# A four-layer fp32 step on one core: the last block's second half of columns gated during the first product, scaling by ScalarE, modulation in smaller turns

## The chip, the core and the metric

The kernel runs on one core of one Trainium2 chip. The metric is device time in microseconds. TensorE (PE in the profile) multiplies matrices out of SBUF into PSUM; VectorE (DVE) and ScalarE (ACT) read and write SBUF and PSUM; GpSimd (POOL) does small things and issues some DMAs; SyncE (SP) issues most DMAs from one queue, in order.

## The reference

One inference step of a backbone of four layers on 128 context tokens and 512 latent tokens, width 1024, in float32. Layer l uses a mixer of kind l mod 3: gated linear attention (GLA, layers 0 and 3), a Conformer convolution (layer 1), a short gated convolution (layer 2). Every layer ends with an MLP.

```
for l in range(4):
    mp, ms = adaln(c_ctx, mod_w[l], mod_b[l]), adaln(c, mod_w[l], mod_b[l])   # 6 vectors of 1024 each: silu(c) @ w + b
    hp, hs = xp * (1 + mp[1]) + mp[0], xs * (1 + ms[1]) + ms[0]
    op, os = mixer_l(hp), mixer_l(hs)
    xp = layer_norm(ALPHA * xp + mp[2] * op);  xs = layer_norm(ALPHA * xs + ms[2] * os)
    fp = square(relu(modulate(xp, mp[3], mp[4]) @ w1[l])) @ w2[l]             # width 4096; the same for xs
    xp = layer_norm(ALPHA * xp + mp[5] * fp);  xs = layer_norm(ALPHA * xs + ms[5] * fs)
```

The outputs are both streams after the last layer and the final states of the GLA scan for the context.

## The kernel before

**Tokens and tiles.** The 640 tokens are five row tiles of 128 (`TT = 5`; tile 0 is the context), which stay in SBUF as `x[t]`. The input of a product stands transposed in `hT`, as two float32r parts, high and low; each weight is split the same way (`split`: a cast on ScalarE, L118, a subtraction on VectorE, L119), and a product is three matmuls, high by high, high by low, low by high. Weights come from HBM through `staged`: five staging buffers of 512 KB (pool `stage`), then the split into weight buffers (pool `wp`, and in a mixer also `wq`, three buffers of each part).

**Order.** PE's instructions run in the order in which the program issues them. The other engines' instructions, the DMA issues on SP among them, are put into a list by a scheduler that goes by the order of the program, readiness in a simulated time, and free buffers; on the chip each engine then runs its list in order. Waits are inserted where data or buffers ask for them.

**MLP.** The 4096 middle columns are done in four blocks `b` of 1024. For each, the first product makes `acts` (in blocks 1 to 3 by a scheme of seven products on half-size forms, `sevens`, L1315, whose forms are built by L118, L119 and L1287), and the second product multiplies them by a block of `w2`, in two halves of 512 columns, `n = 0, 1`. `mm2_wide` goes over a half with five PSUM banks at once, four weights by five row tiles: 20 slots of six matmuls, L208. The results are collected in `x[t]`, whose old value is saved in DRAM after the first block (`saved`). In the last block the epilogue `gathered` adds the collected sum (L264), multiplies by the gate (L265) and adds the saved x (L266), which a DMA on SP brings into one half of the tile `acc` (`room`, L263); the half is `t % 2`, so load t + 2 waits for the addition of tile t. In the last block `n = 0` runs in `mm2_wide`, `n = 1` in `mm2_part`, row tile by row tile (24 matmuls each, L231). The last layer has a plain epilogue, `residual` (L246, L247: multiply by the gate, add), and no saved x; so have the ends of the mixers.

**The norm and the next input.** Behind the epilogue of `n = 1`, `ln` takes the statistics of a row tile (L463, L464, L472, then POOL's L473, L474, L466), normalises the first half of the columns on VectorE (L510) and the second on ScalarE (L512), and registers the rest for 6.2 us of matmul time later (`LN_GAP`): `modulated` transposes the tile on PE (L494, two halves of four), scales it to the next layer's input, the first half on ScalarE (L501), the second on VectorE (L503), and splits it into `hT` (L483, L484).

**Modulation.** The vectors of the next layers are made beside the products. Some groups by PE (`mod_step`), the groups in `MOD_DVE` by VectorE (`mod_dve`): for one vector and one half of its columns, four steps `p`, each with one staged load that holds two k tiles, and per k tile two multiply-adds into `acc` (L400, or ScalarE's L398 at the first). After the last step PE sums over the partitions (L419) and turns the row (L371). Steps are taken by `tick`: some number of times in each `mm2_wide`, and after each group of `sevens`, by `STEPS[l]`; `drain` and `pause` take what is left ahead of a layer's end.

**Opening.** In layer 0 the first modulation comes in eight units (`unit`, two staged loads of 512 KB each); `part_sums` multiplies one (L574), its sums are copied out (L580) and turned (L602), and `products` does the k tile's part of the first GLA products (L679). Unit u + 2 is asked for when unit u has been read. Then come the weights `gvr` of the next products.

## Time and profile before

| | us |
|---|---|
| median of 3 runs | 3017.94 |
| lowest and highest | 3017.71, 3019.01 |
| profiled execution | 3019.96 |
| its span, first to last instruction | 3018.2 |
| mean granted clock of PE in it | 0.988 |

The busy times are shares of the span. The granted clock is a share of 2.4 GHz; PE runs at 1.2 or at 2.4 GHz, and a value between is a mean over a stretch. An idle time of PE with a name behind it is a wait; the name is that of the instruction that ended it. The profiled execution is 1.76 us longer than its span and 2.02 us longer than the median.

### The profile page before, as it was taken

How to read it: one execution, taken by the hardware profiler on the slowest of the kernel's cores; microseconds unless marked ns; L12 is line 12 of the kernel's file. 1: busy time of each engine (PE TensorE's matmuls, PEld its weight loads, DVE VectorE, ACT ScalarE, POOL GpSimd, SP SyncE). 2: the span in 40 equal slices, each digit the busy share in tenths (PEclk: the TensorE clock that was granted, in tenths of full speed). 3: DMA queues.
4: the chain of work that ended last, by engine and by line, in shares of the span. 5: the costliest groups of instructions: out<-in, count | busy, mean ns of one | idle time of the engine just before them, and what ended most of it. 6: DMA issues, size and time to landing. Idle time of an engine off the chain costs nothing.

```text
span 3018.2 us, 42986 instructions
## 1 busy us (share of the span) xinstructions
PE 2913.3 (97%) x16988; PEld 2551.2 (85%) x16988; DVE 2114.7 (70%) x3399; ACT 1212.6 (40%) x1974; POOL 204.3 (7%) x379
## 2 busy tenths in 40 slices
PE   7999999999999999999999999999999999999998
PEld 6788798888788698998889989888988887988996
DVE  4444779798787775776788578877775447685676
ACT  4333354352442353533533234534533443533442
POOL 0001100100110010000010010010010000000000
PEclk9999999999999999999999999999999999999999
DMA  6334244444455334323435324444333312212222
GB/s 248 122 123 157 74 161 136 156 136 162 161 161 148 110 112 139 110 90 124 149 115 170 101 70 142 135 140 133 115 117 128 105 57 74 87 67 84 91 70 77
DMA packets 110809, 366.46 MB, mean 121 GB/s; under 512 B 14996, under 2 KB 20796, under 8 KB 110608
## 3 DMA queue, kind: packets, MB, share of 16 engines
q1 hardware_dynamic: 98656, 333.92, 33.7%
q0 software_dynamic: 11952, 29.80, 3.1%
q8 instruction: 134, 2.20, 0.3%
q14 instruction: 67, 0.55, 0.1%
HBM read 348.55 MB, written 15.11 MB: 120 GB/s over the span
## 4 chain that ended last, share of the span: by engine, by line
PE 81%; DVE 11%; DMA 3%; ACT 2%; issue 2%; POOL 0%; SPq 0%; DVEq 0%; ACTq 0%; POOLq 0%
PE mx L208 14%; PE mm L231 11%; PE mm L208 9%; PE mx L165 9%; PE mx L1315 9%; PE mm L165 9%; PE mm L1315 6%; PE mx L231 5%; DVE acc L400 2%; DVE form L119 1%; DVE wlo L119 1%; PE mx L1090 1%; PE md L346 1%; DMA st<-in_w 1%; PE o L885 1%
## 5 line engine op out<-in xcount | busy, mean ns | idle before, releaser
L118 ACT CAST whi<-st 128x1024 fp32r<-128x1024 f32 (+1 forms) x262 | 273.9, 1050 | 654.8 <-PE mx L208 115.6
L119 DVE TENSOR_TENSOR wlo<-st,whi 128x1024 fp32r<-128x1024 f32 (+1 forms) x262 | 318.8, 1220 | 267.4 <-ACT whi L118 266.4
L208 PE MATMUL mx<-whi,act 128*128 128x512 f32 x1344 | 453.2, 391 | 0.0
L118 ACT CAST form<-st 128x512 fp32r<-128x512 f32 x336 | 201.1, 619 | 371.9 <-DVE st L1287 167.1
L208 PE MATMUL mm<-whi,act 128*128 128x512 f32 x896 | 313.6, 391 | 0.5 <-DVE x L247 0.5
L208 PEld LDWEIGHTS mx<-whi,act 128*128 128x128 f32 x1344 | 252.6, 188 | 57.6 <-issue 4.2
L231 PE MATMUL mm<-whi,hT 128*128 128x512 f32 x920 | 296.9, 395 | 0.0
L119 DVE TENSOR_TENSOR form<-st,form 128x512 fp32r<-128x512 f32 x336 | 224.9, 686 | 93.8 <-ACT form L118 93.4
L400 DVE SCALAR_TENSOR_TENSOR acc<-st,cm,acc 128x512 f32<-128x512 f32 x392 | 276.0, 746 | 19.3 <-ACT acc L398 13.6
L165 PE MATMUL mm<-hT,whi 128*128 128x256 f32 (+1 forms) x1264 | 277.7, 310 | 0.0
L165 PE MATMUL mx<-hT,whi 128*128 128x384 f32 (+1 forms) x1216 | 270.1, 311 | 4.2 <-ACT hT L483 2.4
L208 PE MATMUL mx<-wlo,act 128*128 128x512 f32 x672 | 262.1, 390 | 0.0
L1315 PE MATMUL mx<-hT,form 128*128 128x320 f32 x1428 | 232.3, 311 | 12.9 <-DVE form L119 6.1
L1315 PEld LDWEIGHTS mx<-hT,form 128*128 128x128 f32 x1428 | 215.0, 189 | 18.7 <-DVE form L119 8.8
L165 PEld LDWEIGHTS mm<-hT,whi 128*128 128x128 f32 x1264 | 211.7, 190 | 2.1 <-issue 1.0
L165 PEld LDWEIGHTS mx<-hT,whi 128*128 128x128 f32 x1216 | 205.2, 189 | 6.7 <-ACT hT L483 3.2
L208 PEld LDWEIGHTS mm<-whi,act 128*128 128x128 f32 x896 | 168.2, 188 | 37.5 <-issue 2.1
L231 PEld LDWEIGHTS mm<-whi,hT 128*128 128x128 f32 x920 | 171.5, 188 | 33.4
L165 PE MATMUL mm<-hT,wlo 128*128 128x256 f32 (+1 forms) x632 | 195.2, 309 | 0.5 <-DVE wlo L119 0.5
L165 PE MATMUL mx<-hT,wlo 128*128 128x384 f32 (+1 forms) x608 | 188.6, 310 | 0.0
L231 PE MATMUL mm<-wlo,hT 128*128 128x512 f32 x460 | 183.9, 400 | 0.0
L208 PE MATMUL mm<-wlo,act 128*128 128x512 f32 x448 | 174.8, 390 | 0.0
(313 smaller groups left out, 5183.8 us busy)
## 6 DMA issues: line engine op xcount, KB each, us to landing
st<-in_w SPq DMA_DIRECT2D x256, 512.0 KB, 3.4
st<-in_modv SPq DMA_DIRECT2D x112, 512.0 KB, 3.4
st<-in_modw SPq DMA_DIRECT2D x80, 512.0 KB, 4.5
st<-in_gvr SPq DMA_DIRECT2D x32, 512.0 KB, 5.1
st<-in_cpw SPq DMA_DIRECT2D x24, 512.0 KB, 5.7
st<-in_scin SPq DMA_DIRECT2D x24, 512.0 KB, 4.1
ur<-uscr SPq DMA_DIRECT2D x40, 238.0 KB, 5.4
st<-in_gqk SPq DMA_DIRECT2D x16, 512.0 KB, 5.3
```

Of the source, the lines that this page charges most:

```text
L118: self.nc.scalar.copy(hi, src)
L119: self.nc.vector.tensor_tensor(out=lo, in0=src, in1=hi.bitcast(F32), op=AL.subtract)
L165: self.nc.tensor.matmul(ps[:m, :n], w[a][:, kt * m:(kt + 1) * m], self.hT[:, h, kt, c0:c0 + n], start=(i == 0), stop=(i == 3 * KT - 1),)
L208: self.nc.tensor.matmul(ps[t], lhs(2 * i + k, h, t), s[a][:, k * 512:k * 512 + 512], start=(i == 0 and k == 0 and a == 0 and h == 0), stop ...
L231: self.nc.tensor.matmul(ps, lhs(kt, h, t), s[a][:, c + cols.start:c + cols.stop], start=(i == 0), stop=(i == 3 * nk - 1))
L346: nc.tensor.matmul(ps[32 * t:32 * t + 32, :], self.cm[:, kt, :], st[t // 2][:, c:c + 512], start=(kt == 0), stop=(kt == KT - 1),)
L400: nc.vector.scalar_tensor_tensor(out=acc[:, s], in0=w, scalar=c, in1=acc[:, s], op0=AL.mult, op1=AL.add)
L885: nc.tensor.matmul(o[t], Ep[i][:, t * 128:(t + 1) * 128], ss[i], start=False, stop=((m, i) in ((2, 1), (3, 0), (3, 1))))
L1090: nc.tensor.matmul(ps[32 * g:32 * g + 32, :5 * GRID], w[:, g, q], ur[i][:, g, :, 4 * q:4 * q + GRID], start=(q == 0), stop=(q == 7))
L1315: nc.tensor.matmul(ps, w[c][:, k * 128:(k + 1) * 128], x[:, h, k], start=(i == 0), stop=(i == 11))
```

## The change

1. In the last block of the MLPs of layers 0 to 2, the second half of the columns is gated early: `gather`, a generator stepped between the slots of the first half's `mm2_wide`, multiplies the collected sum of each row tile by the gate and adds the saved x. Behind the second half's product stands the plain epilogue. The first half keeps `gathered`.
2. In those MLPs ScalarE scales both halves of a row tile to the next layer's input (`by_act`).
3. A step of `mod_dve` takes one k tile (two multiply-adds) instead of two; there are eight to a half vector, every second one with a load. `STEPS` doubles, and the short convolution's `mm1` ticks twice for each tick before.
4. Units 1 to 7 of the opening are loaded into the weight buffers of `wq`, not into staging, and unit u + 3 is asked for when unit u has been read.

```diff
-STEPS = {0: (6, 1), 1: (3, 0), 2: (6, 0), 3: (0, 0)}
+STEPS = {0: (12, 2), 1: (6, 0), 2: (12, 0), 3: (0, 0)}
...
-                self.tick()
+                for _ in range(turns):
+                    self.tick()
...
+    def gather(self, saved, room):
+        nc = self.nc
+        c = slice(512, 1024)
+        for _ in range(7):
+            yield
+        for t in range(TT):
+            was, xs = room[:, t % 2], self.x[t][:, c]
+            nc.sync.dma_start(was, saved[t][:, c])
+            nc.vector.tensor_tensor(out=xs, in0=xs, in1=self.gate[:, 0 if t == 0 else 1, c], op=AL.mult)
+            nc.vector.tensor_tensor(out=xs, in0=xs, in1=was, op=AL.add)
+            yield
...
-        st = self.staged(self.d["modv"][l, 2 * v + half, p])
+        if p % 2 == 0:
+            self.mst = self.staged(self.d["modv"][l, 2 * v + half, p // 2])
...
-        for i in range(2):
-            w = st[:, i * 512:(i + 1) * 512]
-            for s in range(2):
-                c = self.cm[:, 2 * p + i, s:s + 1]
-                if p == 0 and i == 0:
...
+        w = self.mst[:, p % 2 * 512:(p % 2 + 1) * 512]
+        for s in range(2):
+            c = self.cm[:, p, s:s + 1]
+            if p == 0:
...
-                if half == 0:
+                if half == 0 or by_act:
                     nc.scalar.activation(hf[:, i], src, AF.Identity, bias=b, scale=a)
...
     def unit(self, u):
-        self.units.append([self.staged(self.d["modw0"][u, i]) for i in range(2)])
+        st = []
+        for i in range(2):
+            if u == 0:
+                st.append(self.staged(self.d["modw0"][u, i]))
+                continue
+            t = self.wq.tile([128, 1024], F32, tag=("whi", "wlo")[i], name="unit")
+            self.nc.sync.dma_start(t, self.d["modw0"][u, i])
+            st.append(t)
+        self.units.append(st)
...
-            if u + 2 < KT:
-                self.unit(u + 2)
+            if u + 3 < KT:
+                self.unit(u + 3)
...
         self.unit(1)
+        self.unit(2)
...
-            self.mm1(d["scin"], evac)
+            self.mm1(d["scin"], evac, turns=2)
...
-            residual = self.residual if last else lambda n: self.gathered(n, b, saved, acc)
+            residual = self.residual if last else lambda n: self.residual(1) if (b, n) == (3, 1) else self.gathered(n, b, saved, acc)
...
+                    todo = iter(()) if last else self.gather(saved, acc)
+                    self.by_act = not last
+                    self.out_proj(
+                        d["w2"][l, b], lhs, nxt, last, load=lambda i, src: load(i if i == 0 else 2, src),
+                        residual=None if last else residual, between=lambda: next(todo, None))
+                    self.by_act = False
```

## Rows read from the trace of the kernel before

**Rows 1.** The page, busy time of each engine and its share of the span
```profile
PE 2913.3 (97%) x16988; PEld 2551.2 (85%) x16988; DVE 2114.7 (70%) x3399; ACT 1212.6 (40%) x1974; POOL 204.3 (7%) x379
```

**Rows 2.** Waits of PE, whole span: waited for, us in total, times, longest
```profile
PE tp L494 <- DVE x L510: 15.3, 7, 4.3
...
PE mx L1315 <- DVE form L119: 6.1, 8, 2.7
PE mm L1315 <- DVE form L119: 5.9, 7, 2.1
PE tp L371 <- DVE mrow L423: 5.8, 6, 1.6
PE tp L602 <- DVE part L580: 4.4, 2, 2.4
```

**Rows 3.** Busy time in stretches: engines (instructions), granted clock, DMA share, GB/s
```profile
785.00:806.00 21.00, 21.00 (x94) 17.39 (x93) 8.70 (x9) 9.91 (x12) 4.80 (x9) 1.00 0.70 222
823.00:836.00 13.00, 7.87 (x32) 6.13 (x31) 8.08 (x18) 4.04 (x8) 2.32 (x6) 0.87 0.12 41
1036.00:1090.00 54.00, 54.00 (x264) 45.18 (x263) 39.82 (x69) 26.05 (x55) 6.65 (x16) 1.00 0.15 53
1523.00:1538.00 15.00, 10.31 (x38) 7.99 (x37) 8.37 (x17) 4.04 (x8) 2.34 (x6) 0.77 0.17 53
2218.00:2231.00 13.00, 9.48 (x51) 7.77 (x50) 10.21 (x21) 4.52 (x10) 2.39 (x6) 1.00 0.13 41
```

**Rows 4.** Timeline where layer 0's MLP ends: start, length, engine, line, what, [idle before]
```profile
816.46 21.64 SPq L263 DMA_DIRECT2D acc<-x  x6
...
823.65 0.68 DVE L266 TENSOR_TENSOR x<-acc,mx 128x512 f32<-128x512 f32 x1
...
827.90 0.66 PE L494 MATMUL tp<-ident,x 128*128 128x128 f32 x4 [4.27 <-DVE x L510]
...
829.97 1.48 ACT L501 ACTIVATE hf<-tp,ab 128x128 f32<-128x128 f32 x4
...
830.18 5.38 PE L231 MATMUL mx<-S,act 128*128 128x512 f32 x18
830.57 1.37 DVE L503 TENSOR_SCALAR hf<-tp,ab 128x128 f32<-128x128 f32 x4 [2.10 <-PE tp L494]
...
837.55 4.36 PE L231 MATMUL mx<-S,act 128*128 128x512 f32 x18
```

**Rows 5.** Single lines: ns min/median/max, first and last start, forms
```profile
L266 DVE TENSOR_TENSOR x<-acc,mx x18: 669/680/691, 809.8 to 2236.7; 128x512 f32<-128x512 f32 x18
...
L400 DVE SCALAR_TENSOR_TENSOR acc<-st,cm,acc x392: 733/746/755, 393.6 to 2111.7; 128x512 f32<-128x512 f32 x196
```

**Rows 6.** Timeline of PE after layer 0's boundary, last tile
```profile
858.40 0.66 PE L494 MATMUL tp<-ident,x 128*128 128x128 f32 x4 [1.50 <-ACT x L512]
```

**Rows 7.** Busy time in two stretches of the opening
```profile
10.00:15.00 5.00, 5.00 (x32) 4.78 (x31) 2.46 (x6) 4.40 (x9) 0.00 (x0) 1.00 1.03 413
15.00:20.00 5.00, 1.76 (x17) 0.80 (x15) 3.33 (x9) 5.00 (x10) 0.00 (x0) 1.00 0.91 370
```

**Rows 8.** Timeline of the opening
```profile
19.15 0.64 PE L574 MATMUL md<-st,cm 128*32 128x256 f32 x8 [2.62 <-DMA st<-in_modw]
...
46.74 0.59 PE L679 MATMUL pa<-hT,whi 128*96 128x384 f32 x2
...
47.86 1.05 ACT L118 CAST whi<-st 128x1024 fp32r<-128x1024 f32 x1 [4.57 <-DMA st<-in_gvr]
...
50.55 0.58 PE L602 MATMUL tp<-ident,part 128*128 128x128 f32 x2 [2.01 <-DVE part L580]
...
52.21 0.93 PE L679 MATMUL pa<-hT,whi 128*96 128x384 f32 x2
```

**Rows 9.** Timeline of the SP queue's DMA issues in layer 0's last block
```profile
784.07 0.80 SPq L263 DMA_DIRECT2D acc<-x  x2
785.88 0.33 SPq L132 DMA_DIRECT2D st<-in_w  x1
```

More of the change, by code (lines that the diff above doesn't have):

```diff
@@ L173, in mm1_pass, with mm1 @@
         run(self.mm1_steps(*args))
-    def mm1(self, srcs, evac, lead=4, load=None):
+    def mm1(self, srcs, evac, lead=4, load=None, turns=1):
         m, n = 0, srcs.shape[0]
@@ L277, in mod_queue @@
                     for half in range(2):
-                        for p in range(4):
+                        for p in range(8):
                             self.fill.append((l, g, partial(self.mod_dve, l, v, half, p)))
@@ L392, in mod_dve @@
         acc, ps, mrow = self.acc, self.mps, self.mrow
-        for i in range(2):
-            w = st[:, i * 512:(i + 1) * 512]
-            for s in range(2):
-                c = self.cm[:, 2 * p + i, s:s + 1]
-                if p == 0 and i == 0:
-                    nc.scalar.activation(acc[:, s], w, AF.Copy, scale=c)
-                else:
-                    nc.vector.scalar_tensor_tensor(out=acc[:, s], in0=w, scalar=c, in1=acc[:, s], op0=AL.mult, op1=AL.add)
-        if p < 3:
+        w = self.mst[:, p % 2 * 512:(p % 2 + 1) * 512]
+        for s in range(2):
+            c = self.cm[:, p, s:s + 1]
+            if p == 0:
+                nc.scalar.activation(acc[:, s], w, AF.Copy, scale=c)
+            else:
+                nc.vector.scalar_tensor_tensor(out=acc[:, s], in0=w, scalar=c, in1=acc[:, s], op0=AL.mult, op1=AL.add)
+        if p < 7:
             return
@@ L972, in gla, with out_proj @@
             self.phase_ps = None
-    def out_proj(self, w, lhs, nxt, last, load=None, residual=None):
-        (self.mm2_wide if load else self.mm2)(w[0], lhs, (residual or self.residual)(0))
+    def out_proj(self, w, lhs, nxt, last, load=None, residual=None, between=None):
+        if load:
+            self.mm2_wide(w[0], lhs, (residual or self.residual)(0), between)
+        else:
+            self.mm2(w[0], lhs, self.residual(0))
         self.out_last(w, lhs, nxt, last, load, residual)
```

7 lines of the change are left out of this document (4 added, 3 removed).

## The prediction

> **What bounds the kernel now.** I read the page's busy times first: TensorE (PE) is busy 97% of the span and VectorE (DVE) 70%, ScalarE (ACT) 40% [rows 1]. The change takes no matmul away, so all it can give is a part of what PE does not fill: 3018.2 − 2913.3 = 104.9 us. Whatever makes DVE or ACT faster counts only where PE stands waiting for it.
>
> So the second view is the list of what PE waited for [rows 2]. The largest entry is the transposes of the next layer's input (L494), which wait for the normalised row tile (L510): 15.3 us in 7 waits. Then come the forms of the seven-product step (L1315 waiting for L119, 6.1 + 5.9 us), the turning of a modulation row (L371, 5.8 us) and the opening (L602 waiting for L580, 4.4 us). Matmuls of the wide products with their modulation turns (L208) show next to no wait of their own.
>
> Third, the busy times by stretch show where the largest entry sits [rows 3]. PE idles 13.00 − 7.87 = 5.13 us around 830 us, 15.00 − 10.31 = 4.69 us around 1530 us and 13.00 − 9.48 = 3.52 us around 2225 us: each is the end of an MLP (layers 0, 1, 2). A mixer's end, 1036 to 1090 us, has the same norm and transposes but the plain epilogue of two operations without a load: PE is busy 54.00 of 54.00 us there. The granted clock in the first two stalled stretches is 0.87 and 0.77, so part of those stretches ran at the lower level (1.2 GHz of 2.4); in the third it stayed 1.00.
>
> Fourth, the timeline of the first of them [rows 4]. PE reached the transposes at 827.90 − 4.27 = 823.63 us. The last addition of row tile 0 (L266, reading the saved x from `acc`) began only at 823.65 us, 4.25 us before the transposes could go. The SP queue's loads of that saved x, six of them, were issued over 21.64 us, each waiting for a slot of `acc`. After the stall 18 matmuls took 5.38 us where the same 18 later took 4.36 us.
>
> **The change, part by part.**
>
> *Second half of columns.* Before, each tile of the last block's second product had three DVE operations and a load behind it: add the earlier blocks, multiply by the gate, add the saved x. After, multiply and add of the old sum happen during the first product, in `gather`, and behind the product stand the two operations of the plain epilogue. That removes one operation of about 0.68 us [rows 5] and the wait for a load from each tile's path, and adds one operation per tile: 5 x 0.68 = 3.4 us a layer. The addition is hidden: in the first product's stretch, 785 to 806 us, DVE is busy 8.70 of 21.00 us [rows 3]. If that cover were gone it would cost 10.2 us over three layers. Operations wholly in SBUF at this width are not in the trace; the nearest row, L266 with one operand in PSUM, bounds them at 0.68 us from above, and nothing suggests a much longer one.
>
> Does the stall go? In the trace 4.25 us pass from the start of tile 0's last addition to the transposes [rows 4], so with PE arriving at 823.63 us the addition has to begin by 819.4 us. The program puts the transposes 6.2 us of matmul time behind the product (`LN_GAP`), so that product ended near 817 us. There are thus 2.4 us for the multiplication (0.68 us) and for whatever of the first product's epilogues DVE still has to do. The first product keeps its three operations and its loads, 5 x 3 x 0.68 = 10.2 us less overlap, so DVE will be just about free. I expect most of the stall to go and about 1.0 us to remain per layer (bounds: 0, and the full 3.5 to 5.1 us if the list order keeps the late addition).
>
> *ScalarE scales the second half too.* Four operations of a tile go from DVE (1.37 us) to ACT (1.48 us) [rows 4]. Five tiles, three layers: DVE loses 20.6 us, ACT gains 22.2 us. DVE is the engine on the path, and ACT is busy 4.04 of 13.00 us in the stalled stretch [rows 3], so the exchange is right in direction. It has a price: halves that ran side by side now run one after the other, so a tile's hT is later by about 1.4 us. Behind the scaling on ACT stand the weight splits of the next mixer and the last tile's normalisation, for which PE already waited 1.50 us in layer 0 [rows 6]; that wait can grow to 1.50 + 1.48 us. My 1.0 us per layer is meant to hold this as well. The Trainium skill (ScalarE: Activation LUTs, Rules for kernel authors) says the opposite of this edit: multiply and add belong on VectorE, not ScalarE. The trace agrees only by 0.11 us per four operations; by that rule alone the edit would cost 15 x 0.11 = 1.7 us if ACT were the bound.
>
> *Sum of the boundaries.* Idle 5.13 + 4.69 + 3.52 = 13.3 us. The slow matmuls add 5.38 − 4.36 = 1.0 us in layer 0; layer 1 has the lower clock, so I take 1.0 us again; layer 2 none. 15.3 us less 3 x 1.0 us gives **−12.3 us** (bounds −15.3 and −4).
>
> *Modulation in turns of one k tile.* The same operations (392 of L400 at 0.746 us [rows 5]) in twice as many turns: runs of two instead of four, 1.5 instead of 3.0 us, spread over 12 instead of 6 points of a wide product. In the seven-product steps two turns replace one at the same point, so nothing moves there, and these steps hold most of the waits (12.0 us for forms). In layer 1's MLP 36 turns of two do what 18 turns of four did, less the 8 that are PE's own steps, whose size is unchanged: 28 half turns against 10 whole ones, so 4 whole ones move there from the short convolution, 16 x 0.746 = 11.9 us of DVE in a stretch with room. A turn's load is held over two turns. What can be won is a part of the 12.0 + 5.8 us [rows 2]; what can be lost is a late form of the same size as those that already wait. I take **−1 us** (bounds −6 and +4).
>
> *Opening.* Unit 1 arrives at 19.15 us after a 2.62 us wait, but the DMA engines are full until then, share 1.03 and 0.91 [rows 7, 8], so its arrival does not move by an earlier issue. From unit 2 on PE scarcely waits for a load. What can go is later: ACT stood 4.57 us for the first gvr load, issued late because the units held the staging buffers; the opening's last steps queued behind it, PE waited 2.01 us at 50.55 us, and the next matmuls of one kind took 0.93 us instead of 0.59 us. With units in weight buffers, staging is free for gvr. I count the 2.0 us and about 2 us of slow matmuls as at stake and take **−3 us** (bounds −4 and +2: the gvr splits now need the buffers of units 5 to 7 and wait for PE's reading of them).
>
> **Sum.** −12.3 − 1 − 3 = −16.3 us. The profiled execution took 3019.96 us (span 3018.2), which makes 3003.7 us; it lay 2.02 us above the median of the runs, so on the median's scale the forecast is **3001.6 us**.
>
> **Rivals.**
>
> *ScalarE takes DVE's place.* The last tiles' normalisation and the splits wait behind the extra 1.48 us per tile; half of the boundary gain goes back. For it speaks the 1.50 us wait that already is ACT's; against it ACT's idle share. On the median's scale, 3018 us: 3018 − 6 − 1 − 3 = 3008 us. Chance 0.16.
>
> *The stalls stay.* DVE's list is still in an order that puts later epilogues ahead of tile 0, or the first product's loads, which now must wait for `gather` to free `acc`, are late and everything behind them too. Only a third of the boundary gain and none of the opening's remains: 3018 − 4 = 3014 us. Chance 0.11.
>
> *Slower: the SP queue.* Loads leave SP in order, and ten of them now wait there for a slot of `acc` earlier than before. In the trace the last weight load of the second product goes out at 785.88 us, right behind the first two loads of saved x at 784.07 us [rows 9]. If SP stands on a slot, that weight and the next mixer's stand behind it. It decides from about 20 us of delay on, since that product starts near 811 us (817 less 24 matmuls at 4.36 / 18 us); a wait as long as the worst seen, 21.64 us for six loads [rows 4], would reach it. Price: a product 5 us late in each of three layers, and no gain at the boundary: 3018 + 15 − 4 = 3029 us. Chance 0.08.
>
> *More than I count:* waits for forms and turned rows also fall by half: 3018 − 15 − 9 − 4 = 2990 us. Chance 0.05.
>
> **How the numbers follow.** My forecast, with 2994 to 3007 us around it, has 0.60. A measurement of this kernel can tell a change from none at about 0.2%, 6 us. Faster by more than that, below 3012 us: 0.60 + 0.05 + most of the first rival and a part of the second, 0.77. Within it: 0.14. Slower: 0.09, the SP case and its milder forms. The range 2991 to 3014 us takes in the first two rivals and leaves out the SP case and the far end of the best one.
>
> **What would show it.** Right: in the three stretches PE's waits for L510 fall from 4.3, 4.3 and 3.5 us to under 1.5 us and the granted clock stays at 1.00; gather's two operations lie inside the first product; the opening's wait at 50.55 us is gone. Wrong: a wait of PE for ACT (hf, hT or the last tile's normalisation) above 2 us at a boundary, PE waiting for weights behind loads of saved x, or more waits for forms in the seven-product steps.

## The result and the profile after

The changed kernel takes 2982.41 us (median of 3 runs, 2981.84 to 2987.29) against 3017.94: a ratio of 0.9887, interval 0.9868 to 0.9907, or 35.5 us less. The forecast was 16.3 us less, with a range that ended at 2991. The direction was right; the gain was more than twice what was counted, and the time lies below the range. In the comparisons below, single runs of the kernel before lie between 3009.5 and 3023.5 us (31 runs) around a median of 3018.0, so a few microseconds in one profile are no finding.

The page of the changed kernel, span and busy times:

```profile
span 2980.6 us, 43001 instructions
...
PE 2897.3 (97%) x16988; PEld 2545.5 (85%) x16988; DVE 2102.5 (71%) x3354; ACT 1230.1 (41%) x2034; POOL 200.4 (7%) x379
```

The gain of 37.6 us between the two profiled spans has two halves. PE's idle time was 104.9 us and is 2980.6 − 2897.3 = 83.3 us: 21.6 us less. The other 16.0 us are busy time, 2913.3 − 2897.3 [rows 1], of the same 16988 matmuls: the mean granted clock rose from 0.988 to 0.992. As the lower level is half of the higher, that is 2 x 0.012 x 3018 = 72 us at 1.2 GHz before and 2 x 0.008 x 2981 = 48 us after; half of that time is lost, so the clock gives 12 of the 16.0 us, and with the rounding of the two means, 1.5 us each, 9 to 15. That holds for this pair of profiles. Over the runs the clock gives less: its median is 0.989 in 83 runs of the kernel before, taken beside the experiments, against 0.991, 0.992 and 0.991 in the three runs of the changed kernel. By the medians that is (0.011 x 3018) − (0.009 x 2982) = 6 us, 3 to 9 with the rounding. Waits that go away take slow matmuls behind them along.

What PE waited for after the change (us in total, times, longest):

```profile
PE mm L1345 <- ACT form L119: 7.5, 3, 3.7
PE md L600 <- DMA st<-in_modw: 6.5, 2, 6.1
PE tp L386 <- DVE mrow L438: 5.9, 7, 1.0
PE tp L509 <- DVE x L525: 5.7, 4, 2.5
PE mx L1345 <- DVE form L120: 5.7, 5, 2.7
PE md L600 <- DMA unit<-in_modw: 4.3, 3, 2.2
PE tp L629 <- DVE part L606: 3.3, 1, 3.3
```

The lines have moved (L494 is L509, L510 is L525, L1315 is L1345, L400 is L415). The transposes' wait for the normalised tile fell from 15.3 us to 5.7 us against [rows 2]. No entry names a weight load of an MLP, and none names ScalarE's scaled tile at an MLP's end.

To see where the time came from, I put the two traces side by side: the k-th matmul of a line before against the k-th of the same line after, and at the bounds of each stage the difference of their start times. The stage's gain is the growth of that difference.

| stage (in the trace before, us) | gain, us |
|---|---|
| opening, 0 to 62 | 3.1 |
| layer 0, MLP, 400 to 812 | −0.2 |
| layer 0, MLP's end, 812 to 866 | 7.65 |
| Conformer, 866 to 1040 | 2.2 |
| layer 1, MLP, 1112 to 1512 | 9.35 |
| layer 1, MLP's end, 1512 to 1568 | 7.13 |
| short convolution, 1568 to 1745 | 3.7 |
| layer 2, MLP, 1830 to 2212 | 0.9 |
| layer 2, MLP's end, 2212 to 2262 | 3.07 |
| all other stages together | 0.7 |

So the three ends give 17.85 us, layer 1's MLP 9.35, the short convolution 3.7, the opening 3.1. The table sets one profile against one, and the stages are not equally firm. The ends repeat within 0.1 us wherever the same parts stand in them, and layer 1's MLP within 1 us. The Conformer does not: in the kernels of the experiments its gain lies anywhere between −1.7 and 4.3 us. The opening is taken up further down.

Stretches of the changed kernel: the first product in layer 0's last block, and the three ends of MLPs (length, busy time with instructions of PE, PEld, DVE, ACT, POOL, then granted clock, DMA share, GB/s):

```profile
783.00:804.00 21.00, 21.00 (x94) 17.38 (x93) 11.69 (x14) 12.13 (x15) 4.77 (x9) 1.00 0.88 290
815.00:828.00 13.00, 11.93 (x57) 9.69 (x56) 8.58 (x17) 5.17 (x12) 2.37 (x6) 1.00 0.18 61
1500.00:1515.00 15.00, 13.93 (x70) 11.46 (x69) 9.52 (x19) 7.86 (x20) 3.29 (x9) 1.00 0.01 2
2183.00:2196.00 13.00, 11.93 (x62) 9.77 (x61) 8.29 (x15) 6.41 (x15) 2.37 (x6) 1.00 0.00 0
```

The first row is `gather`'s cover: DVE busy 11.69 us where it was 8.70 [rows 3], PE full all through. It holds only a part of `gather`, as the experiments show further down. In each of the other three PE idles 1.07 us where it idled 5.13, 4.69 and 3.52 us [rows 3], and the clock stays at 1.00.

Timeline of the changed kernel at the three ends (start, length, engine, line, what, idle before):

```profile
817.60 0.66 DVE L249 TENSOR_TENSOR x<-x,mx 128x512 f32<-128x512 f32 x1
818.19 0.68 DVE L268 TENSOR_TENSOR x<-acc,mm 128x512 f32<-128x512 f32 x1
...
821.77 0.67 DVE L249 TENSOR_TENSOR x<-x,mm 128x512 f32<-128x512 f32 x1
822.36 0.54 DVE L525 TENSOR_SCALAR x<-x,mv 128x512 f32<-128x512 f32 x1
...
822.96 1.09 PE L509 MATMUL tp<-ident,x 128*128 128x128 f32 x8 [1.07 <-DVE x L525]
...
1505.52 1.09 PE L509 MATMUL tp<-ident,x 128*128 128x128 f32 x8 [1.07 <-DVE x L525]
...
2187.97 1.09 PE L509 MATMUL tp<-ident,x 128*128 128x128 f32 x8 [1.07 <-DVE x L525]
```

PE now reaches the transposes at 822.96 − 1.07 = 821.89 us, so by the prediction's 4.25 us tile 0's addition has to begin by 817.64 us; it begins at 817.60 us, just in time. A wait of 1.07 us stays because the path from there to the transposes is 822.96 − 817.60 = 5.36 us, not 4.25: an addition of the first half's epilogue (L268) stands ahead of the statistics, and tile 1's addition ahead of the normalisation.

### The profile page after: what moved, and what is told of

Its sections match the earlier page's. It is cut to its first block, busy times and chain, and to the rows that moved or that the text cites. A ratio compares the mean times of both kernels' runs of the same rounds, so it can differ in the third digit from the quotient of the medians.

```text
span 2980.6 us, 43001 instructions
## 1 busy us (share of the span) xinstructions
PE 2897.3 (97%) x16988; PEld 2545.5 (85%) x16988; DVE 2102.5 (71%) x3354; ACT 1230.1 (41%) x2034; POOL 200.4 (7%) x379
## 4 chain that ended last, share of the span: by engine, by line
PE 86%; DVE 8%; DMA 2%; ACT 2%; issue 2%; POOL 0%; SPq 0%; DVEq 0%; ACTq 0%; POOLq 0%
PE mx L210 14%; PE mm L233 12%; PE mx L166 10%; PE mm L166 10%; PE mm L210 9%; PE mx L1345 9%; PE mm L1345 6%; PE mx L233 5%; DVE acc L415 1%; PE md L361 1%; DVE form L120 1%; PE tp L509 1%; PE o L912 1%; DMA st<-in_w 1%; DVE st L1317 1%
## 5 line engine op out<-in xcount | busy, mean ns | idle before, releaser
L415 DVE SCALAR_TENSOR_TENSOR acc<-st,cm,acc 128x512 f32<-128x512 f32 x392 | 276.3, 745 | 11.6 <-DMA st<-in_modv 6.2
L1345 PE MATMUL mx<-hT,form 128*128 128x320 f32 x1428 | 231.0, 311 | 8.6 <-DVE form L120 5.7
L1345 PEld LDWEIGHTS mx<-hT,form 128*128 128x128 f32 x1428 | 215.4, 189 | 11.9 <-DVE form L120 7.0
```

What stands on the lines that cost most here:

```text
L415: nc.vector.scalar_tensor_tensor(out=acc[:, s], in0=w, scalar=c, in1=acc[:, s], op0=AL.mult, op1=AL.add)
L1345: nc.tensor.matmul(ps, w[c][:, k * 128:(k + 1) * 128], x[:, h, k], start=(i == 0), stop=(i == 11))
```

## The experiments

Labels with e_ are parts of the change put into the kernel before, x_ the changed kernel without a part, d_ more turns put into the seven-product stretches, c_ and g_ variants that move turns or `gather`'s work. The short diffs show the lines that make the run; `...` stands for lines left out, which are those of the diff of the change. Ratios stand against runs of the kernel before on the same chip, with the 95% interval; differences in us from the changed kernel are differences of medians.

| kernel | median us | ratio | interval |
|---|---|---|---|
| e_gather | 3007.57 | 0.9974 | 0.9962 to 0.9987 |
| e_byact | 3020.72 | 1.0012 | 1.0003 to 1.0022 |
| e_mods | 3010.30 | 0.9976 | 0.9966 to 0.9985 |
| e_units | 3012.16 | 0.9985 | 0.9974 to 0.9995 |
| x_byact | 2990.76 | 0.9912 | 0.9898 to 0.9927 |
| e_gather_byact | 3001.29 | 0.9945 | 0.9931 to 0.9960 |
| x_mods | 2999.71 | 0.9943 | 0.9929 to 0.9958 |
| x_units | 2990.03 | 0.9905 | 0.9888 to 0.9921 |
| e_steps4 | 3009.71 | 0.9978 | 0.9967 to 0.9989 |
| e_mods_t3 | 3008.97 | 0.9975 | 0.9963 to 0.9986 |
| c_14_1 | 2983.67 | 0.9883 | 0.9869 to 0.9898 |
| c_mm1 | 2999.20 | 0.9937 | 0.9922 to 0.9952 |
| d_whole | 3027.89 | 1.0031 | 1.0020 to 1.0042 |
| d_half | 3024.32 | 1.0023 | 1.0012 to 1.0033 |
| c_late | 3006.42 | 0.9961 | 0.9945 to 0.9978 |
| g_pin | 2988.41 | 0.9904 | 0.9891 to 0.9916 |
| g_pin_gather | 2996.91 | 0.9935 | 0.9922 to 0.9949 |
| g_pin_14_1 | 2986.41 | 0.9893 | 0.9880 to 0.9906 |

Gains by stage, from the same matching of matmuls as above, in us. Each column is one profiled run; for e_gather that run took 3001.2 us, against the median of 3007.6:

| stage | after | e_gather | e_byact | e_mods | x_byact | e_gather_byact | x_mods | g_pin | g_pin_gather |
|---|---|---|---|---|---|---|---|---|---|
| layer 0, MLP | −0.2 | −1.5 | 0.1 | −1.9 | −1.4 | −2.3 | −4.2 | −2.2 | 2.1 |
| layer 0, end | 7.65 | 7.62 | −2.89 | −0.29 | 7.62 | 7.64 | 7.65 | 7.62 | 7.62 |
| layer 1, MLP | 9.35 | −3.5 | 0.8 | 9.4 | 9.2 | −2.8 | −4.1 | 9.6 | 0.7 |
| layer 1, end | 7.13 | 0.53 | 0.45 | 0.13 | 1.72 | 7.12 | 7.12 | 6.84 | 3.78 |
| short convolution | 3.7 | 3.6 | 3.0 | 1.3 | 3.6 | 3.7 | 3.7 | 3.7 | 3.3 |
| layer 2, end | 3.07 | 2.93 | −3.38 | −1.34 | 3.24 | 3.05 | 3.05 | 2.25 | 2.91 |

**Each part alone.**

*Gathering alone* (e_gather):

```
+    def gather(self, saved, room):
...
-            residual = self.residual if last else lambda n: self.gathered(n, b, saved, acc)
+            residual = self.residual if last else lambda n: self.residual(1) if (b, n) == (3, 1) else self.gathered(n, b, saved, acc)
```

> The kernel before with only the gathering of the last block's second half during the first product. Theory A (each part's gain sits where its code is): the three stalls at the MLP ends lose most of their 13.3 us and the lower clock behind them, time 3018 - 12 = 3006 us, PE's waits for L510 at the three ends under 2 us each. Theory B (VectorE's scaling is just as much to blame): half of it, 3012 us. Theory C (any edit rearranges the lists of VectorE and SP, and the gain outside the ends comes with it): 2995 us or less, with waits for forms in the seven-product steps changed too.

Measured: 10.4 us faster. The ends of layers 0 and 2 gain 7.62 and 2.93 us, all that the whole change gains there; that of layer 1 gains 0.53. The timeline of PE at that end, last tile:

```profile
1547.30 0.83 PE L508 MATMUL tp<-ident,x 128*128 128x128 f32 x4 [2.71 <-DVE x L524]
1548.76 1.11 PE L508 MATMUL tp<-ident,x 128*128 128x128 f32 x4 [0.63 <-ACT x L526]
```

The first tile's stall has fallen to 1.07 us here too, but the last tile is now late by 2.71 + 0.63 us, and slow matmuls follow. In layer 1 a stall was moved, not removed.

*ScalarE's scaling alone* (e_byact):

```
-                if half == 0:
+                if half == 0 or by_act:
...
+                    self.by_act = not last
```

> The kernel before with only ScalarE's scaling of both halves at the MLP ends. Theory A: the late addition stays, so the stall of tile 0 stays (4.3, 4.3 and 3.5 us); at most 2 us are won at later tiles, 3016 us. Theory B: 3012 us. Theory C: 3005 us or less, or slower, with a gain far from the MLP ends.

Measured: 2.7 us slower, the only part that loses alone. PE's waits for the tile that ScalarE normalises, in the kernel before and then in this one:

```profile
PE tp L494 <- ACT x L512: 3.5, 5, 1.5
```

```profile
PE tp L495 <- ACT x L513: 7.3, 6, 3.0
```

They doubled, and the wait for DVE's half stayed (14.4 us against 15.3): the last tiles' normalisation stands behind the scaling, as the first rival had it.

*Smaller turns alone* (e_mods):

```
-STEPS = {0: (6, 1), 1: (3, 0), 2: (6, 0), 3: (0, 0)}
+STEPS = {0: (12, 2), 1: (6, 0), 2: (12, 0), 3: (0, 0)}
...
-                        for p in range(4):
+                        for p in range(8):
...
+            self.mm1(d["scin"], evac, turns=2)
```

> The kernel before with only VectorE's modulation in turns of one k tile. Theory A: what was won between the MLP ends, 9 us in layer 1's MLP, 2 in the Conformer, 4 in the short convolution, comes from here, 3018 - 14 = 3004 us; the stalls at the MLP ends stay at 4.3, 4.3 and 3.5 us. Theory C: the gain between the ends is an accident of the lists, and this part by itself gives between -5 and +5 us.

Measured: 7.7 us faster, with 9.4 us in layer 1's MLP and nothing won in layer 0's (−1.9).

*Units in weight buffers alone* (e_units):

```
+            t = self.wq.tile([128, 1024], F32, tag=("whi", "wlo")[i], name="unit")
...
-            if u + 2 < KT:
-                self.unit(u + 2)
+            if u + 3 < KT:
+                self.unit(u + 3)
```

> The kernel before with only the opening's units in weight buffers. Theory A: 3 us, 3015 us, all of it ahead of 60 us. Theory C: the lists further on change as well, and the time lies elsewhere between 3005 and 3025 us.

Measured: ratio 0.9985, 1.5 to 7.8 us faster by its interval. The opening gains 2.8 us in its profile, but kernels without this part gain there too. Up to 62 us, the ten other kernels that load the units as before are 0.5 to 3.2 us shorter than the profile of the kernel before, 2.0 in the mean, and the nine with the units in weight buffers 2.5 to 3.9 us, 3.1 in the mean. So the profile of the kernel before had a slow opening, and the units are worth about 1 us there.

**Each part left out.**

*Without ScalarE's scaling* (x_byact), the changed kernel with

```
-                if half == 0 or by_act:
+                if half == 0:
```

> The changed kernel without ScalarE's scaling of the second halves (VectorE does them again). Theory A (with the early gathering in place the scaling is what frees VectorE at the MLP ends, so the two work together although scaling alone won nothing): slower than the changed kernel by 5 us or more, about 2990 us. Theory B (the scaling is worth nothing here either): the changed kernel's time within 3 us, 2980 to 2985 us.

Measured: 8.4 us slower than the changed kernel, with intervals that just overlap (0.9898 to 0.9927 against 0.9868 to 0.9907); what the part does is seen in the stages. The end of layer 1 gains 1.72 us where it gained 7.13; layers 0 and 2 lose nothing.

*Gathering and scaling together* (e_gather_byact), the kernel before with parts 1 and 2:

```
+    def gather(self, saved, room):
...
+                if half == 0 or by_act:
```

> The kernel before with the early gathering and ScalarE's scaling, without the other two parts. Theory A: the three MLP ends give all of the changed kernel's 18 us there, 3018 - 18 = 3000 us, so 7 us or more beyond the gathering alone. Theory B: no more than the gathering alone, 3007 us.

Measured: 16.9 us faster than before, 6.3 us more than gathering alone; the end of layer 1 gains 7.12 us. The scaling is worth nothing where DVE alone sets the end (e_byact) and 6 to 8 us where the gathered columns have taken the first stall away and DVE's backlog reaches the last tile.

*Without the smaller turns* (x_mods), the changed kernel with

```
-STEPS = {0: (12, 2), 1: (6, 0), 2: (12, 0), 3: (0, 0)}
+STEPS = {0: (6, 1), 1: (3, 0), 2: (6, 0), 3: (0, 0)}
...
-                        for p in range(8):
+                        for p in range(4):
```

> The changed kernel with the modulation in turns of two k tiles again. Theory A (the smaller turns hold what was won between the MLP ends): 2982 + 12 = 2994 us. Theory C (what was won there belongs to no part): within 4 us of the sum of the other parts' own effects, or anywhere between 2985 and 3000 us with waits at places that have no modulation turn.

Measured: 17.3 us slower than the changed kernel, the most of the three parts that were left out. The gathering was not left out by itself. In layer 1's MLP the difference is 9.35 + 4.05 = 13.4 us. PE's waits there in x_mods, and then in the changed kernel:

```profile
PE mm L1345 <- ACT form L119: 3.0, 2, 1.8
PE mx L1345 <- ACT form L119: 3.0, 1, 3.0
PE tp L386 <- DVE mrow L438: 2.8, 1, 2.8
PE mx L1345 <- DVE form L120: 2.2, 1, 2.2
```

```profile
PE mm L1345 <- ACT form L119: 1.2, 1, 1.2
PE tp L386 <- DVE mrow L438: 0.8, 1, 0.8
PE mx L1345 <- DVE r L1350: 0.4, 1, 0.4
PE mm L1345 <- DVE form L120: 0.4, 1, 0.4
```

Forms and turned rows, in this stage: what the rival "more than I count" named.

*Without the units* (x_units), the changed kernel with

```
-            if u + 3 < KT:
-                self.unit(u + 3)
+            if u + 2 < KT:
+                self.unit(u + 2)
```

and all units in staging again.

> The changed kernel with the opening's units in staging buffers again. Theory A: 3 to 6 us slower, 2986 to 2988 us, all of it ahead of 60 us. Theory C: a difference of other size, and elsewhere.

Measured: 7.6 us slower by the medians, but the intervals overlap (0.9888 to 0.9921 against 0.9868 to 0.9907). The opening itself gains 0.9 instead of 3.1 us; a wait of the same kind as before is back, in the timeline of x_units and then in that of the changed kernel at the same step:

```profile
50.93 0.44 PE L620 MATMUL tp<-ident,part 128*128 128x128 f32 x2 [1.49 <-DVE part L598]
```

```profile
48.83 0.38 PE L629 MATMUL tp<-ident,part 128*128 128x128 f32 x2
```

The other 5 us of the medians have no place outside the opening but differences of 1 to 4 us (the Conformer −1.7 against +2.2); they are within what single profiles scatter and stay open.

**Why the smaller turns pay.** Two reasons were possible: that each turn is short, or that fewer multiply-adds (L400) land in the seven-product stretches. Of the three such stretches of layer 1's MLP, one view counts L400 alone (length, then its busy time and count on DVE, granted clock, DMA share, GB/s). The kernel before; its last line is a stretch of layer 3, which makes no modulation, and behind it stands the same stretch with the busy time of PE, PEld, DVE, ACT and POOL:

```profile
1211.70:1264.80 53.10, 5.89 (x8) 0.97 0.32 102
1320.20:1371.50 51.30, 2.90 (x4) 1.00 0.31 103
1427.60:1483.60 56.00, 8.46 (x12) 0.97 0.40 126
...
2691.80:2740.90 49.10, 0.00 (x0) 1.00 0.29 96
...
2691.80:2740.90 49.10, 49.10 (x337) 49.10 (x336) 42.53 (x75) 28.58 (x48) 0.00 (x0) 1.00 0.29 96
```

The changed kernel (L415):

```profile
1200.50:1249.90 49.40, 0.00 (x0) 1.00 0.29 95
1306.10:1358.00 51.90, 5.80 (x8) 1.00 0.33 107
1413.40:1462.50 49.10, 0.00 (x0) 1.00 0.31 98
```

A stretch without such operations lasts 49.1 to 49.4 us; with 8 of them 51.9 or 53.1 us, with 12 of them 56.0 us. The two longest ran in part at the lower clock (0.97). The sum of the three fell from 160.4 to 150.4 us, which accounts for the 9.35 us of the stage. Between them stand the wide products, where PE is full all through in layer 1, with 20 operations in e_mods and 26 in d_whole. Four kernels try that from both sides.

*More turns in the wide products, none smaller* (e_steps4), the kernel before with

```
-STEPS = {0: (6, 1), 1: (3, 0), 2: (6, 0), 3: (0, 0)}
+STEPS = {0: (6, 1), 1: (4, 0), 2: (6, 0), 3: (0, 0)}
```

> The kernel before with one number changed: four modulation steps of two k tiles in each wide product of layer 1's MLP instead of three. Theory A1 (what the smaller turns won in layer 1's MLP, 9 us, came from their number: the eight steps of PE are done a block earlier, so VectorE's steps are all done ahead of the last seven-product stretch): 3018 - 9 = 3009 us, with no L400 in that stretch. Theory A2 (it came from the smaller grain): 3018 us within 4.

Measured: ratio 0.9978, and 6.6 us in layer 1's MLP. Four operations are left in each of the three stretches, which last 52.0, 51.4 and 50.3 us. One number in a table gives most of what the smaller turns gave there.

*Smaller turns, half as many in layer 1's wide products* (e_mods_t3), e_mods with

```
-STEPS = {0: (12, 2), 1: (6, 0), 2: (12, 0), 3: (0, 0)}
+STEPS = {0: (12, 2), 1: (3, 0), 2: (12, 0), 3: (0, 0)}
```

> The kernel before with the smaller turns, but as many ticks in layer 1's MLP as before (3), so that only the grain is smaller there and the work comes later. Theory A1: nothing won in layer 1's MLP, 3018 us within 4 there, with L400's successor still in the last seven-product stretch. Theory A2: the 9 us are there, 3009 us.

Measured: ratio 0.9975, and 13.2 us in layer 1's MLP, more than the changed kernel gains there: 4, 0 and 4 operations, 50.9, 49.1 and 49.8 us. Theory A1 of this run, that work done earlier is what pays, is thus wrong: here it is done later, and fewer operations are left for the stretches. Its total is that of e_mods all the same; the 3.8 us more in this stage are lost again in pieces of 1 us or so.

*More turns put into the stretches*, whole ones in the kernel before (d_whole) and half ones in e_mods (d_half):

```
-STEPS = {0: (6, 1), 1: (3, 0), 2: (6, 0), 3: (0, 0)}
+STEPS = {0: (6, 1), 1: (3, 1), 2: (6, 0), 3: (0, 0)}
```

> The kernel before with one more modulation step, of two k tiles, after each pair of layer 1's seven-product steps. Theory A3 (a seven-product stretch takes 47 us without VectorE's modulation in it, and about 0.5 us more for each modulation operation that lands in it): its stretches with 12 to 16 such operations take 53 us or more, although more steps are done and the number of ticks rises; 3018 us or slower, against 3010 us for four steps in each wide product. Theory A1 (more steps, earlier, is better): 3010 us or faster.

```
-STEPS = {0: (12, 2), 1: (6, 0), 2: (12, 0), 3: (0, 0)}
+STEPS = {0: (12, 2), 1: (6, 2), 2: (12, 0), 3: (0, 0)}
```

> The kernel before with the smaller turns, and two more of them after each pair of layer 1's seven-product steps: the same operations in the stretches as in the run before, at the smaller grain. Theory A3: the same loss, 3018 us or slower, against 3010 us for the smaller turns alone. Theory A2 (the grain is what counts): 3010 us within 4.

Measured: both slower than before, by 0.31% and 0.23%. The stretches of d_half (its L401 alone):

```profile
1209.40:1263.10 53.70, 10.03 (x14) 1.00 0.37 121
1319.20:1372.70 53.50, 11.63 (x16) 1.00 0.40 128
1428.10:1482.80 54.70, 10.21 (x14) 1.00 0.42 137
```

Stretches with small turns and 14 to 16 operations take 53.5 to 54.7 us; with whole turns and 11, 14 and 17 (d_whole) 51.7, 53.8 and 54.9 us. At 14 operations that is 53.7 and 54.7 against 53.8 us, so there the size of the turn makes no difference. With 4 and 8 operations the smaller turns' stretches are the shorter ones by about 1 us (49.8 and 50.9 against 50.3 to 52.0; 51.9 against 53.1), so most of the gain comes from the count and a little may come from the size. The count alone does not give the length, though. The last stretch of the kernel before takes 56.0 us with 12, of which 8 are steps that `pause` forces at its end, and g_pin_14_1, a kernel of the last group, has two stretches in layer 0 that take 11 and 12 operations almost without loss:

```profile
498.30:548.50 50.20, 7.84 (x12) 1.00 0.41 133
...
726.30:776.30 50.00, 7.57 (x11) 1.00 0.40 133
```

So where in the stretch the operations come counts as well; no run takes that apart. What holds in every kernel looked at is the other end: without such operations a stretch takes 49.1 to 49.5 us.

The total of d_whole is no clean comparison, as PE also waits for a column sum that the same `pause` takes:

```profile
1491.10 1.08 PE L419 MATMUL md<-acc,ones 128*32 128x256 f32 x8 [10.79 <-DVE acc L400]
```

**Can layer 0 have the same?** Its stretches hold 14, 17 and 16 operations before and 14, 15 and 14 after, and its MLP gained nothing. Three versions of the changed kernel move turns out of them.

*More in the wide products* (c_14_1):

```
-STEPS = {0: (12, 2), 1: (6, 0), 2: (12, 0), 3: (0, 0)}
+STEPS = {0: (14, 1), 1: (6, 0), 2: (12, 0), 3: (0, 0)}
```

> The changed kernel with layer 0's modulation turns moved from the seven-product steps (2 to 1 each) into the wide products (12 to 14 each). If VectorE's modulation in the seven-product stretches is what PE waits for (theory A1's mechanism), layer 0's MLP gives 3 to 8 us: 2975 to 2979 us. If the wide products have no room left for it, 2982 us or slower.

Measured: 2983.67 us, no difference from the changed kernel that can be told. The stretches now hold 9, 13 and 11 operations and take 50.1, 55.7 and 53.0 us against 55.1, 54.2 and 58.0, so the second is longer with fewer operations, and the wide product between the last two, now with 46 operations, took 63.6 us where it had taken 59.8. There the room seems to end.

*Sixteen turns in the first block's first product of layer 0* (c_mm1):

```
+            self.every, self.upto = (1, (nl, 2)) if l == 0 else (0, (0, 0))
...
+                    self.mm1(srcs, evac, lead=4 if b == 0 else 1, load=load if b == 0 else None, turns=2)
```

with `STEPS` 0: (13, 0).

> The changed kernel with layer 0's modulation turns out of the seven-product steps altogether: 16 in the first block's first product, 13 in each wide product. By the same mechanism 6 to 12 us, 2970 to 2976 us. If the turns delay the norm's additions at the MLP's start, up to 5 us slower than the changed kernel.

Measured: 2999.20 us, 17 us slower than the changed kernel. Of the last two stretches, which now hold 8 and 6 operations, the last is shorter (51.2 us against 58.0) and the other is not (54.4 against 54.2 with 15 operations). The MLP as a whole loses 1.9 us against the changed kernel's and the step from mixer to MLP ahead of it 5.4 us more: there PE now waits 3.3 and 2.9 us for `hT` (L498, L499) where it waited 1.2 and 0.9. The rest of the 17 us lies in the Conformer, layer 2's MLP and other stages in pieces of 3 us and less, and has no cause that I can show.

*Turns in the evacuations of the first block* (c_late):

```
+                if b == 0 and m >= 4 and l in (0, 2):
+                    self.steps(4)
```

with `STEPS` 0: (13, 0) and 2: (8, 0).

> The changed kernel with VectorE's modulation of layers 0 and 2 taken out of the seven-product steps: 16 turns in the second half of the first block's first product, 13 and 8 in each wide product. Theory A3: the five stretches that now take 54 to 58 us fall towards 50 us; 2982 - 12 = 2970 us. If the operations leak into the stretches all the same, because the wide products are full, 2978 us or slower.

Measured: 3006.42 us. The last stretches of layer 0 have 8 and 6 operations and last 54.4 and 51.2 us, the same as in c_mm1. The MLP of layer 0 loses 8.3 us against the changed kernel's, about as much as two new waits in the timeline of PE:

```profile
446.60 1.08 PE L434 MATMUL md<-acc,ones 128*32 128x256 f32 x8 [5.21 <-DVE acc L415]
...
450.54 1.12 PE L386 MATMUL tp<-ident,mrow 128*128 128x128 f32 x4 [2.86 <-DVE mrow L438]
```

With many turns in a row the sum over partitions and the turned row, which PE takes in its fixed order, come up before DVE has made them; the same two waits stand in layer 2 (5.21 and 2.13 us at 1833 us), whose MLP loses 3.3 us. The profiled run took 2997.3 us; what the median loses beyond it is not shown. Where a turn goes is thus bound from both sides.

**Where `gather` runs.** Two things were open: why the smaller turns are worth 7.7 us alone and 17.3 beside the gathering, and why layer 0's last stretch is no shorter with 14 operations than with 16. `gather`'s multiplications (L280) need no load, so they were issued as soon as the sum was there. The timeline of DVE in the changed kernel, layer 0:

```profile
723.43 0.69 DVE L280 TENSOR_TENSOR x<-x,gate 128x512 f32<-128x512 f32 x1
...
728.24 1.29 DVE L280 TENSOR_TENSOR x<-x,gate 128x512 f32<-128x512 f32 x2
...
787.77 1.29 DVE L281 TENSOR_TENSOR x<-x,acc 128x512 f32<-128x512 f32 x2
```

The additions lie in the first product, from 787.77 us on; all five multiplications lie in the last seven-product stretch, 723.20 to 781.20 us. In layer 1 they begin at 1409.24 us, around the start of the last stretch. With whole turns three are inside it, beside the 12 modulation operations; the window of e_gather for this line alone:

```profile
1417.40:1474.00 56.60, 2.06 (x3) 0.94 0.40 130
```

Three kernels queue the multiplications on DVE behind the last square of the last seven-product step:

```
+            with self.tc.issue_after(self.last_square):
-            nc.vector.tensor_tensor(out=xs, in0=xs, in1=self.gate[:, 0 if t == 0 else 1, c], op=AL.mult)
+                nc.vector.tensor_tensor(out=xs, in0=xs, in1=self.gate[:, 0 if t == 0 else 1, c], op=AL.mult)
```

*In the kernel with gathering alone* (g_pin_gather):

> The kernel before with gathering alone, and the multiplications held behind the last square as in the run above. With gathering alone layer 1's MLP was 3.5 us longer than in the kernel before, with three multiplications beside the 12 modulation operations of its last stretch (56.6 us) and a turned row that PE waited for (2.0 us). Theory: these three made it; layer 1's MLP comes back to within 1 us of before, and the kernel gains 3 us or more over gathering alone (3007.6 us). Rival: the loss is the modulation's own and varies from run to run; the MLP stays 3 us long.

Measured: 2996.91 us, 0.9935 (0.9922 to 0.9949) against 0.9974 (0.9962 to 0.9987) for e_gather. Layer 1's MLP goes from −3.5 to 0.7 us and its end from 0.53 to 3.78, layer 0's MLP from −1.5 to 2.1. So the early multiplications made that loss. The table's stages price it only roughly, as other stretches scatter within them: 1.5 of the 4.2 us in layer 1's MLP lie in the stretch at 1320 to 1371 us, ahead of the multiplications. In the last stretches, where they run, and the first matmuls behind them, the three kernels that have them beside whole turns (e_gather, e_gather_byact, x_mods) lose 1.9, 2.8 and 2.8 us in layer 1 and 3.2, 4.1 and 5.2 us in layer 0; g_pin_gather gains 0.7 and 0.0 us there. That prices them at 2.6 to 3.5 us in layer 1 and 3.2 to 5.2 us in layer 0, and 3.3 us more at layer 1's end where DVE does the scaling.

*In the changed kernel* (g_pin):

> The changed kernel with the gate multiplications of gather queued on VectorE behind the last square of the last seven-product step, so that they run in the first product that follows. In the changed kernel all five of them run in layer 0's last seven-product stretch (723 to 730 us, beside 14 modulation operations; that stretch lasts 58.0 us). Theory: an operation there costs what a modulation operation costs, so the stretch falls to about 55 us and the kernel gains some 3 us in layer 0, 0 to 1 us in layer 1 (two of five lie in the stretch) and nothing in layer 2 (its last stretch has room). Rival: the multiplications, early in the stretch, filled idle time of VectorE; the stretch stays at 58 us, and moved into the first product they make gather's additions late: the ends of the MLPs lose up to 1 us each.

Measured: 2988.41 us (2987.06 to 2990.04), no gain; its interval overlaps the changed kernel's. The last stretch of layer 0 fell from 58.0 to 56.5 us, half of what was expected, and PE has a new wait in the first product behind it:

```profile
PE mx L233 <- DVE x L268: 2.0, 1, 2.0
```

There the held multiplications delay the epilogues of the first half, and the matched matmuls of that product lose 2.2 us. My theory for this run was wrong in sum: the mechanism shows in layer 0's stretch, but what it gives is lost behind it.

*With more turns in layer 0's wide products as well* (g_pin_14_1), g_pin with `STEPS` 0: (14, 1).

> Both of the above ideas for layer 0: STEPS 0: (14, 1) and the held multiplications. Theory: its last stretch has 11 modulation operations and no multiplication and falls from 53.0 to about 51.5 us; the kernel is 2 to 5 us faster than the changed one (2982 us). Rival: the wide product ahead of it is the bound with its 46 operations; no difference.

Measured: 2986.41 us (2981.20 to 2986.88). Layer 0's last stretch is down to 50.0 us with 11 operations, and its MLP gains 3.3 us against before, but the total is the changed kernel's within what can be told. No version beats the changed kernel by more than the intervals.

## Why the prediction was wrong in size

*The boundaries (−12.3; measured −17.85).* The mechanism held as told: the late load and the third operation go, tile 0's addition begins early enough, about 1.0 us stays (1.07 in each), the clock stays at 1.00. The term was mis-sized because it counted the stalled stretch alone and 1.0 us of slow matmuls in two layers. The matched stages also hold the later tiles' waits (the 1.50 us of [rows 6] is gone) and all slow matmuls behind them. Over the three of them PE's idle time fell from 16.43 to 3.65 us, by 12.8 where 13.3 less 3.0 had been counted, and the busy time of the same matmuls from 143.5 to 138.4 us, by 5.1 where 2.0 had been counted; the upper bound, 15.3 us, had left the rest out as well.

*ScalarE's scaling.* The prediction held it for right in direction. Alone it is wrong in direction (ratio 1.0012), by the wait that it had named: 3.5 us grew to 7.3. Together with the gathering it is needed in layer 1 only, for the last tile, and gives 6 to 8 us by the medians (5.4 to 6.6 us in that stage). The Trainium skill (ScalarE: Activation LUTs, Rules for kernel authors) puts multiply and add on VectorE. The loss of 2.7 us in e_byact agrees with it; x_byact goes the other way by 8.4 us, as at that end VectorE is the engine that PE waits for (2.7 us at the longest in x_byact, against 1.07 us). The rule is one of throughput, and the measurement decides: what counts is which engine has the longer list in front of the next transposes.

*The modulation (−1, bounds −6 and +4).* **This is the step that failed:** "In the seven-product steps two turns replace one at the same point, so nothing moves there". The sum went by the size of a turn and by the 4 whole turns that come from the short convolution, "in a stretch with room". Half of that held: the wide products had the room. But layer 1's `STEPS` has no turn in the seven-product steps at all; the operations that stood in them before, 8, 4 and 12, were late ones and those that a forced step takes ahead of the layer's end, and with more done in the wide products they are gone from two stretches of three. DVE is busy 42.5 of 49.1 us in such a stretch without them (layer 3, before), so 12 operations of 0.746 us, 9.0 us, are more than the 6.6 us that are left. This is an estimate that says where to look; g_pin_14_1 shows that it is no hard bound. That count was in the trace of before and wasn't taken. Even 4 of them, 3.0 us, which would fit, cost 1 to 3 us (e_steps4, e_mods_t3), probably as a form then waits for its place in the list. The term measured 9.35 us in layer 1's MLP (PE idle 8.2 us before and 3.2 after, and 4.4 us less busy time for the same matmuls), 7.7 us alone and 17.3 us beside the other parts; what was argued of forms that "already wait" was right in mechanism and put at a tenth.

*`gather` hidden in the first product.* Half right: the additions are, the multiplications run in the last seven-product stretch, where an operation costs. Beside whole turns they cost 2.6 to 3.5 us in layer 1's last stretch and 3.2 to 5.2 us in layer 0's; beside smaller turns 1.5 us in layer 0's, and holding them back loses that again one product later (g_pin). The former two, 6 to 9 us, would be most of the difference between the smaller turns' 17.3 us beside the other parts and 7.7 us alone; no run holds them back beside whole turns and ScalarE's scaling, so this sum is argued, not shown.

*The opening (−3; measured −3.1).* The mechanism is as told: the 2.01 us wait at 50.55 us [rows 8] is gone, and from 45 to 62 us every kernel with the units in weight buffers gains 3.5 us. The agreement of the sum is luck. Kernels without this part gain 1.2 to 2.0 us in the same stretch, as the profile of the kernel before was slow there, so the part itself is worth 1.5 to 2.2 us in it and about 1 us in the opening as a whole. New are 4.3 us in 3 waits for units that now come through the weight buffers (`unit<-in_modw`), beside a fall of the waits for the staged ones from 9.8 us in 5 to 6.5 us in 2. What the units give beyond the opening, 1.5 to 7.8 us in all by e_units, has no place in the stages and stays open.

*Not foreseen: the short convolution (3.7 us).* Before, PE waited there for a column sum and a turned row:

```profile
PE md L419 <- DVE acc L400: 1.8, 1, 1.8
PE tp L371 <- DVE mrow L423: 1.6, 1, 1.6
```

After, no wait is left in that stretch. The gain is in e_gather (3.6) and e_byact (3.0), the two that take work from DVE at the end of layer 1's MLP, and hardly in e_mods (1.3) or e_units (0.8): DVE probably starts the mixer with less behind it.

*The rivals.* ScalarE is busy 7.86 of 15.00 us at layer 1's end and PE doesn't wait for it: only without the gathering does that rival show. The stalls did not stay, and no weight load stands behind a load of saved x. "More than I count" (2990 us, chance 0.05) came nearest, in part by another way than it named. Waits for forms and turned rows did not fall by half: over the whole kernel those for forms went from 19.0 to 17.4 us and those for turned rows from 5.8 to 6.2. In layer 1's MLP those for forms fell from 5.5 to 1.6 us, and slow matmuls made up about half of that stage's gain. The forecast had taken what could be won there from the waits alone, without these.

## What to carry to other kernels

Before you price background work on an engine, count how many of its operations fall into each stretch in which that engine has little left, and compare with the room there; moving them was worth more here than making them smaller, and one number in a table gave most of it. The count says where to look; what a stretch then costs has to be measured. A stall at a boundary costs more than its idle time: add the later tiles, the work that starts with a backlog behind it, and the matmuls at the lower clock. Parts of a change that lose alone can be needed once another part has moved the wait, so price them in the state that the other parts leave.

## What was not expected of the hardware

How much of the gain is clock: in the two profiles some 12 of the 37.6 us came from the same matmuls at a higher mean granted clock, 0.992 against 0.988, and about 6 us by the runs, though the waits that went were of 1 to 4 us each. The clock goes with the scatter of one kernel as well: among the 83 runs of the kernel before, those at 0.988 take 3020 us in the mean (10 runs) and those at 0.991 3013 us (12 runs). The prediction's own row shows the rate, 18 matmuls in 5.38 us behind a stall and 4.36 us elsewhere [rows 4]; in e_gather two matmuls of 128x384 behind the late last tile took 0.84 us, and 0.51 us before it. The Trainium skill (TensorE: Matmul & The Clock Gate, Part 1) says that the clock follows how busy PE has been; the traces agree in that the lower level stands behind the stalls (granted clock 0.87 and 0.77 around two of them [rows 3], 1.00 at the same two ends once they have shrunk to 1.07 us).
